# One fp32 transformer block on one core: rotary tables of the queries alone, weight sums from step 10, one context sum put first, and the last group's final sum in two tiles

## The chip, the cores and the metric

The kernel runs on one core of a Trainium2 chip. The metric is device time in microseconds, median of the runs shown; lower is better. Engines are named as in the profile: PE is TensorE (PEld its weight loads), DVE is VectorE, ACT is ScalarE, POOL is GpSimd and SP is SyncE, which only issues transfers. A line number L1079 is line 1079 of the kernel whose profile is shown; behind the place of an edit the changed kernel's lines stand up to six further down.

## The reference

All inputs and outputs are fp32, and the kernel reaches fp32 precision by splitting numbers. Cut to what matters:

```python
D_MODEL, SEQ, CTX_LEN, HEAD_DIM, N_Q_HEADS, N_KV_HEADS = 2048, 512, 256, 128, 12, 4
h  = modulate(rmsnorm(x, norm_g), shift, scale)         # shift, scale, gate = silu(c) @ w_ada + b_ada
hc = modulate(rmsnorm(ctx, norm_g), shift_c, scale_c)   # 256 context tokens: keys and values alone
kc, vc = rmsnorm(heads(hc @ w_k), k_norm_g), heads(hc @ w_v)
p = h @ w_in                                            # q, k, v, z_a, u_b, z_b, gate_a, gate_b
q = rope(rmsnorm(q, q_norm_g)) * HEAD_DIM ** -0.5
k = rope(rmsnorm(k, k_norm_g))
attn = softmax(q @ cat(k, kc).T) @ cat(v, vc)           # 512 queries, 768 keys, 3 query heads to a key head
y_a = (attn * silu(z_a)) @ w_proj_a
y_b = (fft2(u_b).real * silu(z_b)) @ w_proj_b
out = rmsnorm(x + gate * ((sigmoid(gate_a) * y_a + sigmoid(gate_b) * y_b) @ w_out), final_g)
```

## The kernel before

**One product.** Every number is split in two, hi (rounded, written by ACT, L178) and lo (the rest, subtracted by DVE, L179). `mm3` makes three matmuls of it: hi by hi (L334), lo by hi (L335) and hi by lo (L336).

**One group.** The big products (512 x 2048 by 2048 x 1024 or so) are worked in groups, each as seven half-size products instead of eight, in the order P1, Q5, P2, Q6, P7, Q3, Q4. They use the sums A11, Z5, A12, S2, S3, S4 and A22 of the tokens' quarters and weights that are sums of quarters as well (L272). A product has four pieces of weights. It runs into an accumulator in PSUM: "a" and "c" are pairs of banks with the tag x, "b" has the tag y. Between products DVE and ACT subtract the accumulators into the SBUF tiles X, Y and V (`sub`, L1079), and `done` passes a finished quarter on. In the last group of the input projection (LAST, number 7) the final sum is Y = accumulator − Y after Q4, half of the columns at a time.

**The stages.** Start, up to about 137 us: adaLN's vectors (L562, with weights wa that SP's queue loads), the norms of the tokens, the first weights, and the rotary tables. Then the Fourier mixing, the eight groups of the input projection (kinds qz, qz, qz, gate, gate, kv, gate, gate) up to 815 us, attention from 815.7 to about 1010, branch A's groups (10 and 11), and the output groups 8 and 9 up to the end.

**The tables.** `load_rope` loads the rotary table into the form S3's space and the gains of q and k into Z5's. `rotations` multiplies the table by the gains twice, once for queries and once for keys (four DVE operations, L740), into other parts of S3 and Z5, and POOL's queue stores both in `rot_d` (L743). `load_rotations` brings one or the other back into `turning`: that of the queries ahead of the groups, that of the keys at the KV group's P1.

**The context.** The 256 context tokens' keys and values are made in the KV group (number 5) with the same weights: `self.more` puts six matmuls into "y" after each twelve of the group, and at a product's end `more.end` does the context's own subtractions into cxe and ev (L1225).

**Attention** has 48 steps, one for each head and each 128 queries. A step makes scores over 768 keys, their maximum (DVE, L1480), the exponential (ACT, L1482), six transposes (PE, L1498) into one set of banks, a split of these into pth and ptl (ACT copies, DVE subtracts), the division (L1491 and L1492) and the values (256 columns; two transposes L1513, copy L1523, L1524). Into the gaps go products of branch B and at the end the first of branch A, which read weights that were loaded before (filler, DVE L1446). At the steps in SUM_AT, POOL's queue runs a chain of transfers that adds weights of branch A (`weight_sum`).

**What sets the order.** In the start stage the order on PE, ACT and DVE is written by hand. From there on a scheduler orders the instructions of each engine by its own estimates; names of tiles and the buffers that they get come from the program, and waits follow from these. Transfers stay in the order of their queue.

Of the kernel before, what the change touches and what calls it, by code (L numbers as in the profile page):

```python
# [10 lines left out]
F32 = mybir.dt.float32  # L11
F32R = mybir.dt.float32r
ACT = mybir.ActivationFunctionType
ALU = mybir.AluOpType
# [4 lines left out]
P = 128  # L19
# [4 lines left out]
HD = 128  # L24
# [40 lines left out]
NQZ, KV = 3, 5  # L65
# [24 lines left out]
CHUNKS = (0, 2, 1, 3)  # L90
BRANCH_A, BRANCH_B = 10, (6, 7)
A_CHUNKS = ((0, 2), (1, 3))
SUM_AT = (13, 16, 19, 25, 28, 31)
CHAIN_FROM = {BRANCH_A + 1: 3, 8: 2, 9: 2}
A_FORM = {p[0]: (p[1],) for p in PRODUCTS} | {"Q4": ("A12", "A22"), "P2": ()}

# [24 lines left out]
def block_kernel(ctx, tc, xT, ctx_rows, ctx_toks, x, c_row, w_ss, w_gate, vecs, qkg, rope, dft_c, dft_s,  # L121
                 w_start, w_g, w_pab, w_o, final_g, out):
    nc = tc.nc
# [17 lines left out]
    k_d = dsc.tile([NKV, P, KT, HD], F32, name="k_d")  # L141
    cf_d = dsc.tile([4, P, 7, 2, P], F32, name="cf_d")
    v_d = dsc.tile([NKV, P, KT, HD], F32, name="v_d")
    rot_d = dsc.tile([2, P, 2, 4, HD], F32, name="rot_d")
    p7_d = dsc.tile([2, 3, P, 1024], F32, name="p7_d")
    qz_d = dsc.tile([NH, P, 2, 4, HD], F32, name="qz_d")
    b_d = dsc.tile([2, P, 2, T], F32, name="b_d")
# [581 lines left out]
    def load_rope():  # L729
        i = nc.gpsimd.dma_start(by_rows("S3", 0).rearrange("p (a t) d -> p a t d", a=2), rope)  # L730
        with tc.issue_after(i.ins):
            nc.gpsimd.dma_start(by_rows("Z5", 0)[:, 0:4, :], qkg)

    def rotations():

        r, gq = by_rows("S3", 0), by_rows("Z5", 0)
        for i, f in enumerate(("S3", "Z5")):
            o = by_rows(f, 1)
            for a in range(2):
                nc.vector.scalar_tensor_tensor(o[:, 4 * a : 4 * a + 4, :], r[:, 4 * a : 4 * a + 4, :], (HD ** -0.5, 1.0)[i],  # L740
                                               gq[:, None, 2 * i + a, :].broadcast_to([P, 4, HD]),
                                               op0=ALU.mult, op1=ALU.mult)
            nc.gpsimd.dma_start(rot_d[i], o.rearrange("p (a t) d -> p a t d", a=2))  # L743

    def hold():
        held[:] = [None]
# [277 lines left out]
    class Group:  # L1024
# [16 lines left out]
        def steps(self, name):  # L1041

            form, which = next((f, c) for n, f, _, c in PRODUCTS if n == name)
            if name == "Q3" and self.g >= BRANCH_A:
                which = "d"
            start = which not in self.acc
            if start:

                self.acc[which] = Banks() if self.last and which == "c" else pair(self.tags[which])
            a = self.acc[which]  # L1050
            if name == "Q4" and self.last:
                self.finish(a, form)
                return
            if self.more:
                self.more.begin(name)
            for pc in range(self.pieces):
                w = get((name, self.g, pc))

                apart = (self.g, name, pc) in APART
                for i, (k, t) in enumerate((i // 2, i % 2) if not apart else (i % 2, i // 2) for i in range(4)):  # L1060
                    self.mm(a, form, 2 * pc + k, t, w, start and pc == 0 and k == 0,
                            pc == self.pieces - 1 and k == 1, cont=not start)
                    if i % 2:
                        yield
                if self.more:
                    self.more.products(name, which, pc, w, start)
                for f, h, ready in between(self.g, name, pc):
                    if ready:
                        self.forms[f][4 * h : 4 * h + 4] = split_form(whole[f, h])
                    else:  # L1070
                        make_form(f, h)
                job()
                p = None if self.last else context_piece(self.g, name, pc)
                if p:
                    (context_squares if p[0] == "cn" else context_row)(p[1], get(p))
                q = None if self.last else GATE_AT.get((self.g, name, pc))
                if q is not None:
                    use_gate(q, get(("gate", q)), last_split[-1][1])
            sub = lambda o, x, y: nc.vector.tensor_tensor(o, x, y, op=ALU.subtract)  # L1079
            if name == "P1":  # L1080
                self.X = self.new()
                nc.scalar.copy(self.X, a)
            elif name == "Q5":
                self.Y = self.new()
                for t in ((0,), (1,)) if (self.g, name, 3) in APART else ((0, 1),):
                    t = slice(t[0], t[-1] + 1)
                    nc.scalar.copy(self.Y[:, t, :], a[:, t, :])
            elif name == "P2":
                self.done(0, 0, a, None)
            elif name == "Q6":  # L1090
                self.V = self.new()
                sub(self.V, a, self.X)
                sub(self.Y, self.V, self.Y)
                if self.g >= BRANCH_A:
                    sub(self.X, self.V, self.acc["c"])
                    self.done(1, 1, self.X, self.X)
            elif name == "P7" and self.g >= BRANCH_A:
                pass
            elif name == "P7" and self.last:
                for t in range(2):  # L1100
                    sub(self.V[:, t, :], self.V[:, t, :], a[:, t, :])
                self.done(1, 1, self.V, self.V)
            elif name == "P7":
                sub(self.V, self.V, a)
                self.done(1, 1, self.V, self.V)
            elif name == "Q3" and self.g >= BRANCH_A:
                nc.vector.tensor_tensor(self.V, self.V, a, op=ALU.add)
                self.done(0, 1, self.V, self.V)
            elif name == "Q3":
                if not self.last:  # L1110
                    sub(self.X, a, self.X)
                self.done(0, 1, a if self.last else self.X, self.X)
            elif name == "Q4" and self.g == BRANCH_A + 1:
                self.done(1, 0, a, self.Y)
            elif name == "Q4":
                for t in ((0,), (1,)) if (self.g, name, 3) in APART else ((0, 1),):
                    t = slice(t[0], t[-1] + 1)
                    sub(self.Y[:, t, :], a[:, t, :], self.Y[:, t, :])
                self.done(1, 0, self.Y, self.Y)
            if self.more:  # L1120
                self.more.end(name, which)

        def finish(self, a, form):
# [19 lines left out]
    qr = qzp.tile([P, 2048], F32, name="qr")  # L1143
    new_q = lambda: qr[:, :1024].rearrange("p (a h d) -> p a h d", a=2, h=4)
    turning = qr[:, 1024:].rearrange("p (a t d) -> p a t d", a=2, t=4)

    def load_rotations(i, q):
        q.dma_start(turning, rot_d[i])


    sums, stats = small[:, :32], gain.rearrange("p k j -> p (k j)")
# [182 lines left out]
    def next_wide():  # L1334
        turn_wide[0] += 1
        return wide[turn_wide[0] % 3]

    def get_keys(g):
        raw = get(("K", g))
        tk = next_wide() if g else flat(pair("x"))  # L1340
        for t in range(KT):
            nc.tensor.transpose(tk[:, t * P : (t + 1) * P], raw[:, t * P : (t + 1) * P], ident)
        keys = tiles(g)
        split_from(tk[:, :NKEY], *(w[:, :NKEY] for w in keys))
        kv[g] = tuple(keys) + get(("V", g))
# [4 lines left out]
        qs[h] = take((2, T), F32R)  # L1350
        split_from(tq, qs[h][:, 0, :], qs[h][:, 1, :])

    load_rotations(0, nc.gpsimd)
    for g, kind in enumerate(KINDS):
        if g == 3:
            jobs += [lambda: None] * 12 + [context_norm, lambda: None, lambda: None, context_spread]
# [11 lines left out]
        for name in ONE_GROUP:  # L1368
            if (g, name) in ((0, "Q4"), (KV + 1, "P1")):
                assert not any(p[2] == "raw0" for e in ahead for p, _ in e.raws)  # L1370
                load_row(int(g > 0))
            elif (g, name) == (1, "Q5"):
                silu_of_row(0, flat(new_ev()))
            if (g, name) == (0, "P7"):
                raw_pools.remove((rp, 1, "raw0", 1))
            if (g, name) == (0, "Q5"):
                more_hl.append(1)
                look[0] = 4
            elif (g, name) == (KV, "P1"):
                load_rotations(1, nc.scalar)  # L1380
            elif (g, name) == (KV - 1, "Q3"):
                raw_pools.remove((rp, 1, "raw1", 1))
                hl_pools[:] = [p for p in hl_pools if not isinstance(p, int)]
            elif (g, name) == (KV + 1, "Q6"):
                raw_pools += [(rp, 1, "raw1", 1), (gvp, 2, "raw", 2)]
            elif (g, name) == (LAST, "P7"):
                raw_pools.remove((gvp, 2, "raw", 2))
            elif (g, name) == (LAST, "Q3"):

                free += [(fms[i], f"s{i}") for i in (4, 5, 6, 7, 12, 13, 14, 15, 8, 9, 10, 11, 2, 3, 0, 1)]  # L1390
                for h in range(2):
                    load_head(h)
            elif (g, name) == (LAST, "Q4"):
                hl_pools[:] = [p for p in hl_pools if not isinstance(p, int)]
                get_keys(0)
                jobs.append(lambda: turn_queries(0, pair("y")[:, 0, :]))
            group.run(name)
# [613 lines left out]
```

## Time and profile before

| What | Value |
| --- | --- |
| median of the 3 runs shown (lowest, highest) | 1302.36 us (1300.53, 1302.63) |
| profiled execution, its own time | 1303.86 us |
| its span in the profile | 1302.1 us |
| PE busy, share of the span | 1279.2 us, 98% |
| DVE, ACT, POOL busy | 76%, 53%, 13% |
| mean granted clock of TensorE | 0.995 |

Read first how much PE is busy; then its waits, which are short and few; then at each one the timeline, which tells what released it. A timeline row has the start in us, the duration in us, engine, line, operation, out<-in, the count, and in brackets the idle time ahead of it and its releaser. The granted clock is 1.00 where TensorE runs at full speed.

### The profile page before, as it was taken

The numbers are of one execution on the slowest core, as the hardware profiler recorded it, in microseconds if no ns is written. First come the engines' busy times: TensorE is split into PE (matmuls) and PEld (weight loads), VectorE is DVE, ScalarE is ACT, GpSimd is POOL, SyncE is SP. The second block draws the span as 40 slices with busy tenths as digits, with TensorE's granted clock in tenths as the row PEclk, the third lists the DMA queues.
The fourth block names the chain that finished last, engine by engine and source line by source line (L and its number), as shares of the span: only waits on it lengthen the run. The fifth ranks groups of instructions, "written<-read, shape, count | busy, mean of one in ns | idle before, by whom it ended". The sixth has DMA issues, their size and how long they took to land.

```text
span 1302.1 us, 17705 instructions
## 1 busy us (share of the span) xinstructions
PE 1279.2 (98%) x6598; PEld 1052.2 (81%) x6598; DVE 995.7 (76%) x1301; ACT 685.0 (53%) x1076; POOL 169.6 (13%) x223
## 2 busy tenths in 40 slices
PE   8999999999999999999999999999999999999997
PEld 4677988888888888887888888888888888888885
DVE  5667899889679787647687756788889667887676
ACT  5322655545456455444345545666677546464544
POOL 0000011111102111012021010011111211211210
PEclk9999999999999999999999999999999999999998
DMA  9999588988899889977879897477872899998985
GB/s 377 408 381 352 195 223 220 251 219 253 198 315 245 256 282 292 289 198 181 277 203 285 263 234 253 152 227 241 242 237 69 240 246 254 241 210 231 222 203 171
DMA packets 104519, 320.13 MB, mean 246 GB/s; under 512 B 9904, under 2 KB 32944, under 8 KB 100464
## 3 DMA queue, kind: packets, MB, share of 16 engines
q1 hardware_dynamic: 55056, 197.86, 42.1%
q0 software_dynamic: 27200, 98.85, 35.7%
q10 hardware_dynamic: 22176, 22.29, 5.1%
q8 instruction: 52, 0.85, 0.3%
q14 instruction: 35, 0.29, 0.1%
HBM read 283.82 MB, written 35.14 MB: 245 GB/s over the span
## 4 chain that ended last, share of the span: by engine, by line
PE 81%; DMA 8%; DVE 5%; ACT 2%; issue 2%; SPq 0%; ACTq 0%; DVEq 0%
PE banks L334 10%; PE banks L335 10%; PE banks L336 10%; PE x L334 7%; PE x L336 7%; PE x L335 7%; PE y L335 6%; PE y L334 6%; PE y L336 6%; DMA wa<-in_w_ss 3%; PE banks L1498 2%; DMA wr<-in_w_g 2%; PE pd L562 1%; DVE wlo L179 1%; PE pb L334 1%
## 5 line engine op out<-in xcount | busy, mean ns | idle before, releaser
L178 ACT ACTIVATE whi<-R 128x1024 fp32r<-128x1024 f32 x138 | 145.0, 1058 | 137.2 <-PE banks L336 49.1
L179 DVE TENSOR_TENSOR wlo<-R,whi 128x1024 fp32r<-128x1024 f32 x138 | 167.5, 1221 | 51.3 <-ACT whi L178 51.2
L179 DVE TENSOR_TENSOR wlo<-wr,whi 128x1024 fp32r<-128x1024 f32 (+1 forms) x122 | 147.2, 1212 | 70.8 <-ACT whi L178 70.7
L178 ACT ACTIVATE whi<-wr 128x1024 fp32r<-128x1024 f32 (+1 forms) x122 | 127.5, 1051 | 131.2 <-PE y L336 39.2
L334 PE MATMUL banks<-whi,s 128*128 128x512 f32 x396 | 157.4, 398 | 2.4 <-DVE ev L1079 1.5
L335 PE MATMUL banks<-wlo,s 128*128 128x512 f32 x396 | 156.1, 394 | 0.1
L336 PE MATMUL banks<-whi,s 128*128 128x512 f32 x396 | 155.7, 393 | 0.0
L334 PE MATMUL x<-whi,s 128*128 128x512 f32 x352 | 137.2, 390 | 0.0
L336 PE MATMUL x<-whi,s 128*128 128x512 f32 x352 | 137.0, 389 | 0.0
L335 PE MATMUL x<-wlo,s 128*128 128x512 f32 x352 | 136.9, 389 | 0.0
L334 PE MATMUL y<-whi,s 128*128 128x512 f32 x316 | 123.1, 389 | 1.0 <-DVE cxe L1225 1.0
L335 PE MATMUL y<-wlo,s 128*128 128x512 f32 x316 | 123.1, 389 | 0.5 <-DVE wlo L179 0.5
L336 PE MATMUL y<-whi,s 128*128 128x512 f32 x316 | 122.8, 389 | 0.0
L287 POOL DMA_DIRECT2D R<-in_w_g x64 | 56.0, 875 | 413.4 <-DVE wlo L179 241.8
L178 ACT ACTIVATE s<-wr 128x512 fp32r<-128x512 f32 (+2 forms) x93 | 60.3, 677 | 73.6 <-DMA wr<-cf_d 24.0
L179 DVE TENSOR_TENSOR s<-wr,s 128x512 fp32r<-128x512 f32 (+2 forms) x93 | 66.8, 749 | 37.1 <-ACT s L178 36.4
L334 PEld LDWEIGHTS banks<-whi,s 128*128 128x128 f32 x396 | 74.8, 189 | 18.2 <-ACT whi L178 1.9
L336 PEld LDWEIGHTS banks<-whi,s 128*128 128x128 f32 x396 | 74.8, 189 | 15.6
L335 PEld LDWEIGHTS banks<-wlo,s 128*128 128x128 f32 x396 | 74.8, 189 | 14.3 <-DVE wlo L179 0.5
L336 PEld LDWEIGHTS x<-whi,s 128*128 128x128 f32 x352 | 66.1, 188 | 13.9
L334 PEld LDWEIGHTS x<-whi,s 128*128 128x128 f32 x352 | 66.1, 188 | 13.6
L335 PEld LDWEIGHTS x<-wlo,s 128*128 128x128 f32 x352 | 66.1, 188 | 13.5
(321 smaller groups left out, 2826.1 us busy)
## 6 DMA issues: line engine op xcount, KB each, us to landing
wr<-in_w_g SPq DMA_DIRECT2D x128, 512.0 KB, 5.7
R<-in_w_g POOLq DMA_DIRECT2D x64, 512.0 KB, 7.6
wa<-in_w_ss SPq DMA_DIRECT2D x31, 1024.0 KB, 10.2
R<-in_w_g SPq DMA_DIRECT2D x32, 512.0 KB, 5.3
wr<-in_w_gate SPq DMA_DIRECT2D x32, 512.0 KB, 5.1
wr<-in_w_o SPq DMA_DIRECT2D x24, 512.0 KB, 7.2
R<-in_w_o POOLq DMA_DIRECT2D x24, 512.0 KB, 9.2
wr<-in_w_pab SPq DMA_DIRECT2D x20, 512.0 KB, 5.2
```

The source lines that it names most:

```text
L178: first = nc.scalar.activation(hi, src, ACT.Copy)
L179: return first, nc.vector.tensor_tensor(lo, src, hi.bitcast(F32), op=ALU.subtract)
L287: nc.gpsimd.dma_start(chain[e.pc], e.nxt, accum_op=ALU.add)
L334: nc.tensor.matmul(o, ah, bh, start=start, stop=False, skip_group_check=cont)
L335: nc.tensor.matmul(o, ah, bl, start=False, stop=False, skip_group_check=cont)
L336: nc.tensor.matmul(o, al, bh, start=False, stop=stop, skip_group_check=cont)
L562: nc.tensor.matmul(acc[32 * j : 32 * j + 32], c2[:, n, :], w[:, k, :], start=n < 4, stop=n >= KK - 4)
L1498: nc.tensor.transpose(tp[:, k * P : (k + 1) * P], p[:, k * P : (k + 1) * P], ident)
```

## The change

Five edits, of which none takes a matmul away:

1. SUM_AT is earlier: the six chains start at steps 10 to 28 instead of 13 to 31.
2. `rotations` makes the table of the queries alone, in place, from half of the gains, and stores that. At the KV group's P1, ACT's queue loads the raw table and two rows of gains, and at its Q5 two DVE operations (`scale_tables`) make the keys' table of them, behind the last split.
3. At the KV group's Q6 the context's subtraction is called right behind V, ahead of Y.
4. In the group LAST the accumulator "c" is two tiles (`Banks`) instead of one. P7's subtraction goes by halves; the first half of Y is subtracted in Q4's last piece, right after that half's products.
5. The first transposes of the keys (`get_keys`, g = 0) go to a pair of banks with the tag y instead of x.

```diff
-SUM_AT = (13, 16, 19, 25, 28, 31)
+SUM_AT = (10, 13, 16, 19, 25, 28)
...
-    rot_d = dsc.tile([2, P, 2, 4, HD], F32, name="rot_d")
+    rot_d = dsc.tile([P, 2, 4, HD], F32, name="rot_d")
...
-            nc.gpsimd.dma_start(by_rows("Z5", 0)[:, 0:4, :], qkg)
+            nc.gpsimd.dma_start(by_rows("Z5", 0)[:, 0:2, :], qkg[:, 0:2, :])
+    def scale_tables(r, gains, factor):
+        for a in range(2):
+            nc.vector.scalar_tensor_tensor(r[:, a], r[:, a], factor, gains[:, None, a, :].broadcast_to([P, 4, HD]),
+                                           op0=ALU.mult, op1=ALU.mult)
     def rotations():
-        r, gq = by_rows("S3", 0), by_rows("Z5", 0)
-        for i, f in enumerate(("S3", "Z5")):
-            o = by_rows(f, 1)
-            for a in range(2):
-                nc.vector.scalar_tensor_tensor(o[:, 4 * a : 4 * a + 4, :], ...)
-            nc.gpsimd.dma_start(rot_d[i], o.rearrange("p (a t) d -> p a t d", a=2))
+        r = by_rows("S3", 0).rearrange("p (a t) d -> p a t d", a=2)
+        scale_tables(r, by_rows("Z5", 0), HD ** -0.5)
+        nc.gpsimd.dma_start(rot_d, r)
...
-                self.acc[which] = Banks() if self.last and which == "c" else pair(self.tags[which])
+                self.acc[which] = Banks() if (self.last or self.g == LAST) and which == "c" else pair(self.tags[which])
...
+                    if i == 1 and (self.g, name) == (LAST, "Q4") and apart:
+                        nc.vector.tensor_tensor(self.Y[:, 0, :], a[:, 0, :], self.Y[:, 0, :], op=ALU.subtract)
...
             elif name == "Q6":
                 sub(self.V, a, self.X)
+                if self.more:
+                    self.more.end(name, which)
                 sub(self.Y, self.V, self.Y)
...
-            elif name == "P7" and self.last:
+            elif name == "P7" and (self.last or self.g == LAST):
...
-                for t in ((0,), (1,)) if (self.g, name, 3) in APART else ((0, 1),):
-                    t = slice(t[0], t[-1] + 1)
-                    sub(self.Y[:, t, :], a[:, t, :], self.Y[:, t, :])
+                if self.g == LAST:
+                    sub(self.Y[:, 1, :], a[:, 1, :], self.Y[:, 1, :])
+                else:
+                    sub(self.Y, a, self.Y)
...
-            if self.more:
+            if self.more and name != "Q6":
                 self.more.end(name, which)
...
-        tk = next_wide() if g else flat(pair("x"))
+        tk = next_wide() if g else flat(pair("y"))
...
             elif (g, name) == (KV, "P1"):
-                load_rotations(1, nc.scalar)
+                nc.scalar.dma_start(turning, rope)
+                nc.scalar.dma_start(new_q()[:, 0, 0:2, :], qkg[:, 2:4, :])
+            elif (g, name) == (KV, "Q5"):
+                with tc.issue_after(last_split[-1][1].ins):
+                    scale_tables(turning, new_q()[:, 0, 0:2, :], 1.0)
```

DVE at the end of the KV group's Q6, before. The first and third rows are V and Y of the group, L1225 is the context's, and L272 adds weights that a transfer brings:

```order
L1079 TENSOR_TENSOR ev_5034<-y_4684,ev_4681 128x1024
L272 TENSOR_TENSOR wr_5066<-R_1335,wr_5066 128x1024
L1079 TENSOR_TENSOR ev_4795<-ev_5034,ev_4795 128x1024
L1225 TENSOR_TENSOR cxe<-y_4575,ev_4576 128x512
L179 TENSOR_TENSOR wlo_5070<-wr_5046,whi_5069 128x1024
L1225 TENSOR_TENSOR ev_4576<-cxe,ev_4576 128x512
L179 TENSOR_TENSOR wlo_5096<-wr_5066,whi_5095 128x1024
```

And now:

```order
L1081 TENSOR_TENSOR ev_5034<-y_4684,ev_4679 128x1024
L272 TENSOR_TENSOR wr_5066<-R_1332,wr_5066 128x1024
L1227 TENSOR_TENSOR cxe<-y_4572,ev_4573 128x512
L1081 TENSOR_TENSOR ev_4795<-ev_5034,ev_4795 128x1024
L1227 TENSOR_TENSOR ev_4573<-cxe,ev_4573 128x512
L179 TENSOR_TENSOR wlo_5070<-wr_5046,whi_5069 128x1024
L179 TENSOR_TENSOR wlo_5096<-wr_5066,whi_5095 128x1024
```

The context's two operations have each moved up one place: the first stands ahead of Y now, the second ahead of a split.

PE where attention ends, before. `s_8399` is the tile of exponentials that the transposes L1498 read, the rows with `s_8257` are score products, `whi_7925` is the filler and `whi_8014` the first product (P1) of branch A:

```order
L335 MATMUL banks<-s_7916,s_8257 128x256
L334 MATMUL banks<-s_7915,s_8257 128x256
L335 MATMUL banks<-s_7916,s_8257 128x256
L336 MATMUL banks<-s_7915,s_8257 128x256
L1498 MATMUL banks<-ident,s_8399 128x128 x4
L336 MATMUL banks<-s_7915,s_8257 128x256
L334 MATMUL banks<-whi_7925,s_6465 128x512
L335 MATMUL banks<-wlo_7926,s_6465 128x512
L336 MATMUL banks<-whi_7925,s_6466 128x512
L1498 MATMUL banks<-ident,s_8399 128x128
L1498 MATMUL banks<-ident,s_8399 128x128
L334 MATMUL banks<-whi_8014,s_6659 128x512
```

And now, where the same tiles have numbers higher by two:

```order
L335 MATMUL banks<-wlo_7928,s_6467 128x512
L336 MATMUL banks<-whi_7927,s_6468 128x512
L334 MATMUL banks<-s_7917,s_8259 128x256
L335 MATMUL banks<-s_7918,s_8259 128x256
L336 MATMUL banks<-s_7917,s_8259 128x256
L1504 MATMUL banks<-ident,s_8401 128x128 x4
L334 MATMUL banks<-whi_8016,s_6661 128x512
L335 MATMUL banks<-wlo_8017,s_6661 128x512
L336 MATMUL banks<-whi_8016,s_6661 128x512
...
L1504 MATMUL banks<-ident,s_8401 128x128
L1504 MATMUL banks<-ident,s_8401 128x128
```

Between the four transposes and the last two there stood one score matmul and three of the filler; now nine matmuls of P1 stand there (three are shown; the rest repeat them).

ACT at the same place, before. `pth_8410` is the copy of a step's transposes, L1482 the exponentials of steps 46 (`s_8427`) and 47 (`s_8475`), `whi_8501` a split of a weight tile:

```order
L178 ACTIVATE pth_8410<-banks 128x6x128
L1492 ACTIVATE s_8100<-s_8100,gain 128x128
L178 ACTIVATE s_8625<-s_7332 128x512
L1523 COPY R_1335<-banks 128x256
L178 ACTIVATE s_8498<-s_7004 128x512
L178 ACTIVATE s_8454<-s_8371 128x512
L178 ACTIVATE whi_8501<-R_1334 128x1024
L1482 ACTIVATE s_8427,gain<-banks,gain 128x768
L1482 ACTIVATE s_8475,gain<-banks,gain 128x768
L178 ACTIVATE pth_8410<-banks 128x6x128
```

And now:

```order
L178 ACTIVATE pth_8412<-banks 128x6x128
L1488 ACTIVATE s_8477,gain<-banks,gain 128x768
L1529 COPY R_1332<-banks 128x256
L178 ACTIVATE s_8500<-s_7009 128x512
L178 ACTIVATE whi_8503<-R_1331 128x1024
L1488 ACTIVATE s_8429,gain<-banks,gain 128x768
L178 ACTIVATE s_8456<-s_8373 128x512
L178 ACTIVATE pth_8412<-banks 128x6x128
```

The exponential of step 47 has moved from behind that of 46, and from behind the split of the weight tile, to right behind the first of the two copies.

More of the change, by code (lines that the diff above doesn't have):

```diff
@@ L731, in load_rope @@
         with tc.issue_after(i.ins):
-            nc.gpsimd.dma_start(by_rows("Z5", 0)[:, 0:4, :], qkg)
-    def rotations():
-        r, gq = by_rows("S3", 0), by_rows("Z5", 0)
-        for i, f in enumerate(("S3", "Z5")):
-            o = by_rows(f, 1)
-            for a in range(2):
[L740 to L743, printed above, removed]
+            nc.gpsimd.dma_start(by_rows("Z5", 0)[:, 0:2, :], qkg[:, 0:2, :])
[3 more added lines that the diff above has]
+                                           op0=ALU.mult, op1=ALU.mult)
+    def rotations():
+        r = by_rows("S3", 0).rearrange("p (a t) d -> p a t d", a=2)
+        scale_tables(r, by_rows("Z5", 0), HD ** -0.5)
+        nc.gpsimd.dma_start(rot_d, r)
     def hold():
@@ L1145, in block_kernel @@
     turning = qr[:, 1024:].rearrange("p (a t d) -> p a t d", a=2, t=4)
-    def load_rotations(i, q):
-        q.dma_start(turning, rot_d[i])
     sums, stats = small[:, :32], gain.rearrange("p k j -> p (k j)")
@@ L1351, in turn_queries @@
         split_from(tq, qs[h][:, 0, :], qs[h][:, 1, :])
-    load_rotations(0, nc.gpsimd)
+    nc.gpsimd.dma_start(turning, rot_d)
     for g, kind in enumerate(KINDS):
```

## The prediction

> **What bounds the kernel now.** I read the page first, then the waits of TensorE over the whole span, then the timeline around each of its longer waits, and last the windows around the longest. Page, busy time by engine and the chain that ended last:
>
> ```profile
> PE 1279.2 (98%) x6598; PEld 1052.2 (81%) x6598; DVE 995.7 (76%) x1301; ACT 685.0 (53%) x1076; POOL 169.6 (13%) x223
> ```
>
> ```profile
> PE 81%; DMA 8%; DVE 5%; ACT 2%; issue 2%; SPq 0%; ACTq 0%; DVEq 0%
> ```
>
> TensorE is busy for 98% of the span and makes up 81% of the chain. No edit takes a matmul away, so only its waits, and time in which it runs slowly, can go. The waits of TensorE (engine and line, who released it: us in total, times, longest):
>
> ```profile
> PE banks L1498 <- ACT s L1482: 2.0, 1, 2.0
> PE pd L562 <- DMA wa<-in_w_ss: 1.5, 3, 0.5
> PE banks L334 <- DVE ev L1079: 1.5, 1, 1.5
> ```
>
> ```profile
> PE y L334 <- DVE cxe L1225: 1.0, 1, 1.0
> PE banks L334 <- ACT s L1482: 0.7, 2, 0.4
> ```
>
> Four of these lie where the change works: wa (early stage, beside the tables' DMA), cxe (context's Q6), ev (the last group's final sum) and s L1482 (the end of attention). Together that is some 6 us. A change of 0.2% is 2.6 us here, about what a measurement of this kernel can tell from no change.
>
> **Part 1, tables of the queries alone.** Timeline of TensorE at two of the adaLN products that are 64 matmuls long; the first is broken by a load:
>
> ```profile
> 93.50 2.80 PE L562 MATMUL pd<-wa,c 128*32 128x256 f32 x48
> 96.81 1.07 PE L562 MATMUL pd<-wa,c 128*32 128x256 f32 x16 [0.52 <-DMA wa<-in_w_ss]
> ```
>
> ```profile
> 109.39 3.66 PE L562 MATMUL pd<-wa,c 128*32 128x256 f32 x64
> ```
>
> The broken one takes 96.81 + 1.07 − 93.50 = 4.38 us, the whole one 3.66: the wait costs 0.72. What that load shared the DMA engines with (DMA of 78 to 100 us; issues with KB each and us to landing):
>
> ```profile
> DMA packets 1440, 8.03 MB, mean 365 GB/s; under 512 B 162, under 2 KB 162, under 8 KB 759
> ```
>
> ```profile
> rot_d<-S POOLq DMA_DIRECT2D x1, 512.0 KB, 5.0
> rot_d<-Z POOLq DMA_DIRECT2D x1, 512.0 KB, 9.9
> ```
>
> The store of the keys' table (Z) goes, and with it half of the gains, which were loaded earlier. 512 KB over the mean of this stretch (365 GB/s) is 1.4 us of DMA time that the load has to itself, twice the wait; I take the 0.72 off whole (bounds 0 and 1.4). Also gone are two of the four DVE operations at L740, and the rest now write in place:
>
> ```profile
> 77.48 1.29 DVE L740 SCALAR_TENSOR_TENSOR S<-S,Z 128x512 f32<-128x512 f32 x2
> ```
>
> ```profile
> 79.06 0.54 POOL L743 DMA_DIRECT2D rot_d<-S  x1 [17.66 <-DVE S L740]
> ```
>
> ```profile
> 89.77 0.42 DVE L638 TENSOR_TENSOR S<-xt 128x256 f32<-128x256 f32 x1
> ```
>
> That is 1.29 us of DVE, off the path here (no matmul is released by L740): nothing. In-place writing makes form_row's first write (L638 at 89.77) wait for the store of S. Issued at 79.06 and landed after 5.0, the store is done at 84.1, 5.7 us ahead; even with Z's 9.9 it would be done at 89.0. Nothing. The same two operations return in the KV group, in a gap of DVE (timeline of DVE):
>
> ```profile
> 566.67 1.23 DVE L179 TENSOR_TENSOR wlo<-R,whi 128x1024 fp32r<-128x1024 f32 x1 [2.07 <-ACT whi L178]
> ```
>
> The order puts them ahead of this split: 1.29 us into 2.07 of idle time. Without that cover a weight tile's lo half would be 1.29 us later. ACT's queue issues one DMA more, past P1's splits; an issue of this kind takes POOL 0.54 above, and nothing waits for its data before Q5, a product later. Nothing for both.
>
> **Part 2, context's Q6 in front.** Timeline of DVE and then of TensorE:
>
> ```profile
> 611.62 1.23 DVE L272 TENSOR_TENSOR wr<-R,wr 128x1024 f32<-128x1024 f32 x1 [0.58 <-DMA wr<-in_w_g]
> 612.77 1.22 DVE L1079 TENSOR_TENSOR ev<-ev,ev 128x1024 f32<-128x1024 f32 x1
> 613.90 0.68 DVE L1225 TENSOR_TENSOR cxe<-y,ev 128x512 f32<-128x512 f32 x1
> ```
>
> ```profile
> 614.64 0.50 PE L334 MATMUL y<-whi,s 128*128 128x512 f32 x1 [1.03 <-DVE cxe L1225]
> ```
>
> TensorE waits for cxe, and cxe stands behind a 1.22 us operation that nobody on TensorE needs. Swapped, cxe starts at 612.77 and ends at about 613.45; the y matmul, now placed two matmuls earlier, starts at about 613.55, and those two follow it. A matmul here takes 0.226 from one to the next:
>
> ```profile
> 200.00:300.00 100.00, 100.00 (x442) 1.00 0.86 244
> ```
>
> (100 us with 442 matmuls.) The two that used to stand ahead of the wait take 0.45 behind it, so the work done by 614.64 is 614.64 − 613.55 − 0.45 = 0.64 further on: I take 0.7 (bounds 0, if the load that L272 waits for is later by as much, and the whole 1.03). The context's first subtraction now holds the 1.22 us one back by 0.7; what it makes is read after the product, and no matmul waits for it.
>
> **Part 3, the last sum in two tiles.** Timelines of DVE and of TensorE:
>
> ```profile
> 812.67 1.23 DVE L179 TENSOR_TENSOR wlo<-wr,whi 128x1024 fp32r<-128x1024 f32 x1 [1.49 <-ACT whi L178]
> 814.29 1.29 DVE L1079 TENSOR_TENSOR ev<-x,ev 128x512 f32<-128x512 f32 x2 [0.40 <-PE x L336]
> ```
>
> ```profile
> 815.73 0.47 PE L334 MATMUL banks<-whi,s 128*128 128x512 f32 x1 [1.47 <-DVE ev L1079]
> ```
>
> Both halves (1.29 together) are subtracted only after the last matmul, and attention's first matmul waits for both. Now the first half is complete six matmuls (1.36 us) earlier; DVE is free at about 813.85 (operations in a row start some 0.1 before the end of the one ahead, as at 613.90 above), subtracts it until about 814.5, and the second half runs from there to 815.15. With the 0.15 from DVE's end to the matmul that the rows show (814.29 + 1.29 to 815.73), TensorE starts at about 815.25 to 815.3 instead of 815.73: 0.5 (bounds 0 and 1.0, the wait less one half's 0.6 or so). The keys' transposes in "y" change nothing: that tile was read out one group before.
>
> **Part 4, the sums from step 10, and the order of attention.** The sums are six chains of DMAs on POOL, off the path. What they change is which buffer each later step gets, and with that the order that the scheduler writes over the last 20 steps on three engines. The stall there is the kernel's longest. TensorE and ACT around it:
>
> ```profile
> 1000.35 0.82 PE L1498 MATMUL banks<-ident,s 128*128 128x128 f32 x6
> ```
>
> ```profile
> 1007.28 0.44 PE L1498 MATMUL banks<-ident,s 128*128 128x128 f32 x2 [2.03 <-ACT s L1482]
> 1008.16 0.67 PE L334 MATMUL banks<-whi,s 128*128 128x512 f32 x1 [0.44 <-ACT s L1482]
> ```
>
> ```profile
> 1000.94 0.63 ACT L178 ACTIVATE s<-s 128x512 fp32r<-128x512 f32 x1
> 1001.46 0.81 ACT L178 ACTIVATE pth<-banks 128x768 fp32r<-128x768 f32 x1
> ...
> 1005.29 1.06 ACT L178 ACTIVATE whi<-R 128x1024 fp32r<-128x1024 f32 x1 [0.35 <-PE banks L336]
> 1006.25 0.88 ACT L1482 ACTIVATE s<-banks,gain 128x768 f32<-128x768 f32 x1
> ...
> 1007.13 0.89 ACT L1482 ACTIVATE s<-banks,gain 128x768 f32<-128x768 f32 x1
> ```
>
> TensorE waits for two exponentials (steps 46 and 47) that run one after the other behind a split of 1.06 us: 2.03 + 0.44 = 2.47 us. In the new order the scores of 47 are finished before the values of 43, so its exponential follows the copy of step 44's transposes directly, and nine matmuls of the branch's P1 stand before the two transposes that need the other one. I walk it with the durations above; each time in the walk is an estimate. In the new order two splits stand before step 44's copy, so I put it at 1002.2 rather than 1001.46; exponential 47 then ends at about 1003.9, before TensorE comes to P1, which I put at 1005.0 behind the values that changed places. Nine matmuls of 0.226 last until 1007.05; copy, split and the 1.06 us split run until 1005.9, exponential 46 until 1006.8. The stall is gone, with 0.2 us to spare; a later wait for step 45's copy leaves 0.4. And the stall costs more than itself (window of TensorE: us, busy, granted clock, DMA share, GB/s):
>
> ```profile
> 1008.00:1012.00 4.00, 3.84 (x10) 0.57 0.38 22
> ```
>
> After it the granted clock averages 0.57 over four microseconds: 4 x 0.43 = 1.7 us lost. So 2.5 + 1.7 − 0.4 = 3.8 off. Against it I set 0.7 for new small waits in the reordered steps (the 0.4 and 0.3 that attention shows elsewhere now), with bounds of 0 and 4.2, one more stall of the old size.
>
> The Trainium skill, page TensorE: Matmul & The Clock Gate, Part 1: The HAM clock gate, says that the clock halves after an idle window of about 3.4 us, and its summary advises against gaps over about 3. By that rule a gap of 2.5 us would not halve it; the trace shows that it did, and I go by the trace. By the rule alone the 1.7 would stay and the sum be smaller by that.
>
> **Part 5, given back.** The branches that follow load almost without pause (window of TensorE with the DMA share, then ACT and TensorE's weight loads):
>
> ```profile
> 1030.00:1160.00 130.00, 129.41 (x599) 1.00 0.96 241
> ```
>
> ```profile
> 1124.16 1.06 ACT L178 ACTIVATE s<-wr 128x1024 fp32r<-128x1024 f32 x1 [4.03 <-DMA wr<-in_w_o]
> ```
>
> ```profile
> 1127.48 0.19 PEld L335 LDWEIGHTS banks<-wlo,s 128*128 128x128 f32 x1 [0.48 <-DVE wlo L179]
> ```
>
> At 1127.48 TensorE already has no slack: one load late by 1 us makes it wait 1 us. The load is issued when TensorE has freed its buffer, so it moves along with TensorE; I give back 0.5 (bounds 0 and 3.8).
>
> **The sum** against the profiled execution, 1303.86 us (span 1302.1): 0.7 + 0.7 + 0.5 + 3.8 − 0.7 − 0.5 = 4.5 off, 1299.4. The median of the runs shown is 1302.36, so I forecast 1302.36 − 4.5 = 1297.9.
>
> **The rivals.** (1) The end of attention keeps a stall of its size. Between ready and needed lie only 0.2 us in my walk, and any split of 0.6 us that comes later undoes it. Then parts 1 to 3 remain, less 0.2 for later waits: 1302.4 − 1.7 = 1300.7. (2) The gain of attention is given back to the loads of the branches; for it the DMA share of 0.96, against it that loads follow TensorE. 1302.4 − 1.9 + 0.7 = 1301.2. (3) Slower: transposes become the bound of the last steps. There is one set of banks for them, so each step is transposes (0.82), copy (0.81) and this subtraction in series (groups of instructions):
>
> ```profile
> L179 DVE TENSOR_TENSOR ptl<-banks,pth 128x768 fp32r<-128x768 f32 x48 | 45.8, 954 | 12.0 <-ACT pth L178 11.6
> ```
>
> That is 2.6 us of about 4 (48 steps from 815.7 to 1010). The new order on ACT puts an exponential (0.88) and one to two splits (0.63) before that copy; from 1.4 us in front of it on, TensorE waits. Four steps with 1.2 us each, with the half clock of 1.7 after and the old stall's 2.5 + 1.7 in another place, come to 1302.4 − 1.9 − 4.2 + 4.8 + 1.7 + 4.2 = 1307.0. For it: three engines are reordered over 20 steps. Against: ACT idles in this stage between its groups. (4) The clock: if the halving comes from something else than the gap, the 1.7 stay: 1297.9 + 1.7 = 1299.6. For it, that the gap is short; against it, that the clock is whole before the gap and halved right behind it. The rule cited in part 4 would give this case. (5) The change does none of it: the waits reappear one operation on. 1302.4.
>
> **The numbers.** Forecast 0.46; rival 1 0.21; rival 2 0.09; rival 3 0.13; rival 4 0.05; rival 5 0.06. Faster by over 0.2% (below 1299.8): nearly all of the forecast (0.43), the smaller half of rival 4 (0.03), and 0.06 where rivals 1 and 2 come out better than their number: 0.52. Slower (above 1305.0): rival 3, 0.13, and 0.03 of rivals 1, 2 and 5 with a further stall of 4.2: 0.16. Within: 0.32. Below the forecast the bounds of parts 1 to 3 (1.4 + 1.0 + 1.0 against 1.9 taken) and the 1.2 of small waits could bring 2.7 more; I reach down to 1294.9. Upwards the range goes through rivals 1, 2 and 5 to 1305.3 and leaves out most of rival 3. The forecast's own range is 1295.5 to 1300.
>
> **What would show it.** Right: no wait of L1504's transposes on an exponential over 1 us near 1000, a granted clock of 1.00 in the 20 us after, the y matmul waiting under 0.5 us near 612, attention's first matmul under 1.1 us, and no wait on wa near 96. Wrong: any wait of TensorE over 1.5 us between 930 and 1010, or waits on loads in the branches that sum to over 2 us. If attention stalls as now, the forecast is wrong by its largest term; if the early waits stay, only by 2 us.

## The result, and the profile after

The changed kernel takes 1297.12 us (median of 6 runs, 1296.16 to 1297.93) against 1302.92 (median of 6 runs, 1300.53 to 1305.16) before: 5.8 us less, a ratio of 0.9954 with a 95% interval of 0.9943 to 0.9964. The forecast was 1297.9. The profiled execution has a span of 1294.4 us against 1302.1.

The page of the changed kernel, busy time by engine, and the waits of TensorE (us in total, times, longest):

```profile
PE 1276.4 (99%) x6598; PEld 1050.6 (81%) x6598; DVE 994.9 (77%) x1302; ACT 684.6 (53%) x1076; POOL 169.1 (13%) x222
```

```profile
PE pd L543 <- DVE s L541: 3.2, 3, 2.4
PE pc L523 <- DVE eps_t L346: 1.1, 1, 1.1
PE banks L334 <- DVE ev L1081: 1.0, 1, 1.0
PE pd L562 <- DMA wa<-in_w_ss: 0.7, 2, 0.5
...
PE banks L1504 <- DVE ptl L179: 0.4, 1, 0.4
PE banks L334 <- ACT s L1488: 0.4, 1, 0.4
```

The first two rows are waits of the start stage that lie at none of the edits (2.9 and 1.0 before). Of the four waits at the edits, the longest, 2.0 on an exponential, is gone, and the one on cxe is too short to be listed. The wait for the last group's sum went from 1.5 to 1.0, that on wa from 1.5 to 0.7 in all. Now the places one by one. The adaLN product that was broken, and the context's Q6 on DVE and on TensorE:

```profile
93.16 3.66 PE L562 MATMUL pd<-wa,c 128*32 128x256 f32 x64
```

```profile
610.82 0.68 DVE L1227 TENSOR_TENSOR cxe<-y,ev 128x512 f32<-128x512 f32 x1
611.42 1.21 DVE L1081 TENSOR_TENSOR ev<-ev,ev 128x1024 f32<-128x1024 f32 x1
```

```profile
611.14 0.39 PE L336 MATMUL x<-whi,s 128*128 128x512 f32 x1
611.56 0.50 PE L334 MATMUL y<-whi,s 128*128 128x512 f32 x1
```

The product is whole and takes 3.66 us. The context's subtraction stands ahead of the 1.21 us one, and the y matmul follows the x one 0.42 us after its start, where 0.23 is the pace: 0.2 of waiting is left of 1.03. The last group's final sum and attention's first matmul:

```profile
811.14 0.68 DVE L1064 TENSOR_TENSOR ev<-x,ev 128x512 f32<-128x512 f32 x1
811.74 0.68 DVE L1081 TENSOR_TENSOR ev<-x,ev 128x512 f32<-128x512 f32 x1
```

```profile
812.57 0.47 PE L334 MATMUL banks<-whi,s 128*128 128x512 f32 x1 [0.98 <-DVE ev L1081]
```

The first half (L1064) starts right when DVE is free, the second 0.60 later, as in the walk. And the end of attention, on ACT, on TensorE, and as a window of TensorE (us, busy, granted clock, DMA share, GB/s):

```profile
999.00 0.81 ACT L178 ACTIVATE pth<-banks 128x768 fp32r<-128x768 f32 x1
1000.16 0.90 ACT L1488 ACTIVATE s<-banks,gain 128x768 f32<-128x768 f32 x1 [0.36 <-DVE s L179]
...
1002.96 0.90 ACT L1488 ACTIVATE s<-banks,gain 128x768 f32<-128x768 f32 x1
```

```profile
1002.12 0.47 PE L334 MATMUL banks<-whi,s 128*128 128x512 f32 x1
...
1004.28 0.38 PE L1504 MATMUL banks<-ident,s 128*128 128x128 f32 x2
```

```profile
1004.00:1008.00 4.00, 4.00 (x21) 1.00 0.35 30
```

The exponential of step 47 ends at 1001.06, and P1 starts at 1002.12 without a wait. That of 46 ends at 1003.86, and the two transposes behind the nine matmuls start at 1004.28 without a wait, with 0.4 us to spare. The clock stays at 1.00.

**Where the time came from.** Both traces have the same 6598 matmuls, so the start of the n-th in the one less its start in the other tells how far ahead the changed kernel is. A column of the table is what this lead grows by in a stretch (us; the stretches are in times of before), for the kernels of the experiments too, all against the one profiled execution of before:

| Kernel | 88-105 (wa) | 417-432 | 432-599 | 599-623 (Q6) | 782-818 (last sum) | 818-990 | 990-1037 (end of attention) | 1037-1292 |
| --- | --- | --- | --- | --- | --- | --- | --- | --- |
| the change | 0.73 | 0.83 | -0.31 | 1.00 | 0.53 | -0.61 | 4.57 | 0.50 |
| sums alone | 0.12 | 0.74 | -1.75 | 0.31 | 0.03 | -0.27 | 4.45 | 0.08 |
| all but sums | 0.73 | 0.83 | -0.47 | 0.67 | 0.54 | -0.48 | 1.57 | 0.31 |
| sums from 10, last at 31 | 0.37 | -0.25 | -0.15 | 0.15 | 0.04 | -0.41 | -0.07 | 0.46 |
| no tables | 0.44 | 0.83 | -0.01 | 0.91 | 0.54 | -0.37 | 4.56 | -0.72 |
| no Q6 | 0.73 | 0.83 | -0.10 | 0.10 | 0.51 | -0.56 | 4.61 | -0.31 |
| no two tiles | 0.73 | 0.83 | -0.45 | 1.00 | 0.03 | -1.04 | 4.42 | 0.32 |
| last sum at 25 | 0.73 | 0.37 | -0.88 | 1.12 | 0.53 | -1.46 | 4.55 | -0.49 |

Not all of a column is an edit's. The two profiles of before and of the change are 7.7 us apart, where the medians are 5.8 apart. In 432-599 the sums alone lose 1.75, although their edit lies elsewhere, and between 105 and 417, which the table leaves out, three kernels (all but sums, no Q6, last sum at 25) lose 0.7 to 1.2 and the others nothing. At 990 the orders differ, so a few tenths can belong to the column beside.

### The profile page after: what moved, and what is told of

Same layout as the page of the kernel before. It is cut to its first block, busy times and chain, and to the rows that moved or that the text cites. A ratio compares the mean times of both kernels' runs of the same rounds, so it can differ in the third digit from the quotient of the medians.

```text
span 1294.4 us, 17700 instructions
## 1 busy us (share of the span) xinstructions
PE 1276.4 (99%) x6598; PEld 1050.6 (81%) x6598; DVE 994.9 (77%) x1302; ACT 684.6 (53%) x1076; POOL 169.1 (13%) x222
## 4 chain that ended last, share of the span: by engine, by line
PE 95%; DMA 2%; DVE 1%; ACT 1%; issue 0%; SPq 0%; ACTq 0%; DVEq 0%
PE banks L334 10%; PE banks L335 10%; PE banks L336 10%; PE x L336 9%; PE x L334 9%; PE x L335 9%; PE y L334 8%; PE y L335 8%; PE y L336 8%; PE banks L1504 2%; PE pd L562 2%; PE pb L334 2%; PE pb L335 1%; PE pb L336 1%; PE pc L334 1%; PE pc L336 1%
```

## The experiments

**1. Sums alone** (kernel before, one line):

```diff
-SUM_AT = (13, 16, 19, 25, 28, 31)
+SUM_AT = (10, 13, 16, 19, 25, 28)
```

> The kernel before with SUM_AT alone changed. The theory (the sums give attention its new order, and that takes the long stall and the half clock behind it away): faster than before by 3.1 to 4.9 us, no wait of TensorE over 1 us between 930 and 1010, a granted clock of 1.00 there; the waits on cxe (1.0) and on the last group's sum (1.5) stay. The rival (the earlier parts carry the gain, attention's is given back to the loads of the branches): within 1 us of before.

Measured: 1299.20 against 1303.31, 4.1 us less, ratio 0.9963 (0.9951 to 0.9976). Here and below the microseconds are differences of medians, and the ratio is the recorded one, not their quotient; before has runs of its own beside each set of experiments, the change has none. Window of TensorE over the place of the stall:

```profile
1004.00:1014.00 10.00, 10.00 (x65) 1.00 0.29 23
```

No stall, no half clock; the theory's 3.1 to 4.9 holds, and the rival is out. The waits on cxe (0.7 here) and on the last sum (1.5) are there as before.

**2. All but the sums** (the changed kernel):

```diff
-SUM_AT = (10, 13, 16, 19, 25, 28)
+SUM_AT = (13, 16, 19, 25, 28, 31)
```

> The changed kernel with the old SUM_AT. The theory: 1.5 to 2.5 us faster than before (tables 0.7, context's Q6 0.7, last sum 0.5 to 0.65), and the stall of 2.0 + 0.4 us at attention's end stays, with or without half clock behind it. The rival: 4 us or more faster than before.

Measured: 1301.03, 2.3 us less than before, ratio 0.9981 (0.9970 to 0.9993). The stall is there, and this time the clock did not fall (TensorE's timeline, and windows):

```profile
1006.55 0.44 PE L1504 MATMUL banks<-ident,s 128*128 128x128 f32 x2 [2.03 <-ACT s L1488]
1007.43 0.50 PE L334 MATMUL banks<-whi,s 128*128 128x512 f32 x1 [0.44 <-ACT s L1488]
```

```profile
1005.42:1008.83 3.41, 1.83 (x8) 1.00 0.49 37
1008.83:1012.25 3.42, 3.42 (x26) 1.00 0.53 32
```

So the halving does not always follow this stall. By the table's 990-1037 column, the same stall without it costs 1.57 us less than in the profile of before, which had it: the price of the half clock, forecast at 1.7. The two parts add up within the noise: 4.1 and 2.3, against 5.8 for both.

**3. Earlier sums, but the last chain left at step 31** (kernel before):

```diff
-SUM_AT = (13, 16, 19, 25, 28, 31)
+SUM_AT = (10, 13, 16, 19, 25, 31)
```

> The kernel before with the sums at steps 10, 13, 16, 19, 25 and 31: earlier but for the last chain. Theory A (the last chain's step alone sets the order at the end, by the buffers it holds): within 1 us of before, with the stall of 2.0 + 0.4 us. Theory B (it counts that the chains as a whole run earlier, through the transfers): 2 to 4 us faster than before.

Measured: 1303.80 against 1303.31, ratio 1.0000 (0.9991 to 1.0009). The instructions of TensorE, ACT and DVE stand in the order of before, and the stall is back, with half clock behind it:

```profile
1007.30 0.44 PE L1498 MATMUL banks<-ident,s 128*128 128x128 f32 x2 [2.03 <-ACT s L1482]
1008.18 0.50 PE L334 MATMUL banks<-whi,s 128*128 128x512 f32 x1 [0.45 <-ACT s L1482]
```

Theory A holds as to the step: moving the five other chains alone does nothing. This kernel and that of experiment 1 differ only in the last chain: with it at step 28 attention has the new order, with it at 31 the old one. Whether the chain acts by the buffer that it holds for three steps, as the theory says, or by the places of its transfers, no run here tells apart.

**4. Both tables at the start again** (the changed kernel; `load_rope`, `rotations` and the load ahead of the groups as before, too):

```diff
-    rot_d = dsc.tile([P, 2, 4, HD], F32, name="rot_d")
+    rot_d = dsc.tile([2, P, 2, 4, HD], F32, name="rot_d")
...
-                nc.scalar.dma_start(turning, rope)
-                nc.scalar.dma_start(new_q()[:, 0, 0:2, :], qkg[:, 2:4, :])
-            elif (g, name) == (KV, "Q5"):
-                with tc.issue_after(last_split[-1][1].ins):
-                    scale_tables(turning, new_q()[:, 0, 0:2, :], 1.0)
+                load_rotations(1, nc.scalar)
```

> The changed kernel with both tables made and stored at the start, as before. The theory: 5.8 - 0.7 = 5.1 us faster than before, 0.7 slower than the change, with a wait on wa of 0.5 us at about 96 us back. The rival (the tables do nothing, that wait came and went by itself): as fast as the change, 5.8 us faster than before, and no such wait.

Measured: 1298.18, 5.1 us less than before, ratio 0.9955 (0.9942 to 0.9967), which is too wide to tell 0.7 us. The trace does tell (adaLN's product):

```profile
93.25 3.94 PE L562 MATMUL pd<-wa,c 128*32 128x256 f32 x64
```

In all five traces with the new tables this product takes 3.66 us whole. In all four without, the load is late: 3.94 here, 4.38 before, and a lead in the stretch that is smaller by 0.73 (before), 0.61 (sums alone), 0.36 (sums from 10) and 0.29 (here), in the mean 0.5. The wait is real and its size changes from run to run; the full 0.72 was the case of one profile.

**5. Gaps of TensorE by themselves** (the changed kernel; behind its end, 56 times with k from 2 to 8 and n from 40 to 54; the loop's body):

```diff
+                for i in range(n):
+                    nc.tensor.matmul(acc, w, m, start=i == 0, stop=i == n - 1)
+                nc.vector.tensor_copy(c[:, 0:256], acc[:, 0:256])
+                for _ in range(k):
+                    nc.vector.tensor_tensor(c[:, 0:256], c[:, 0:256], one[:, 0:256], op=ALU.subtract)
+                nc.scalar.copy(m[:, 0:16], c[:, 0:16])
```

> The changed kernel with 56 made gaps of TensorE behind its end: runs of 40 to 54 matmuls, and between them a chain of 3 to 9 operations on DVE and one on ACT for which the next matmul waits, so gaps of an estimated 1.5 to 3.5 us. Its time isn't compared. Theory G (the length of one gap decides): sorted by length, the gaps that are followed by half clock lie above one length between 1.4 and 2.5 us, the rest below. Theory W (TensorE's busy share in stretches of 3.41 us, on a grid that runs through the whole execution, decides): gaps of about 2 us have both outcomes, and they are told apart by how much of the grid's stretch was idle, with the boundary at about half. Theory P (the rule of 3.4 us idle): no half clock behind any gap under 3.4 us.

Measured, in one execution: gaps of 1.82 to 4.58 us in steps of 0.46. Half clock followed 4 of 8 gaps of 1.82, 5 of 8 of 2.28, 7 of 8 of 2.74, of 3.20 and of 3.66, and all of the longer ones. The stretches of half clock last 3.41 us or multiples of it, and start on one grid of 3.41 us. Two gaps of the same length (timeline), and the grid's windows around them (us, busy, clock):

```profile
1620.26 12.32 PE L1956 MATMUL sw_acc<-sw_m,sw_w 128*128 128x512 f32 x46 [1.82 <-ACT sw_m L1960]
...
1730.04 11.18 PE L1956 MATMUL sw_acc<-sw_m,sw_w 128*128 128x512 f32 x48 [1.81 <-ACT sw_m L1960]
```

```profile
1617.13:1620.55 3.42, 1.60 (x7) 1.00 0.00 0
1620.55:1623.96 3.41, 3.41 (x9) 0.50 0.00 0
1726.36:1729.78 3.42, 1.87 (x9) 1.00 0.00 0
1729.78:1733.19 3.41, 3.15 (x14) 1.00 0.02 5
```

The first gap lies in one window, of which TensorE was busy for 1.60; the next window runs at half clock. The second is shared by two windows, neither busy for less than 1.87; the clock stays. Over all windows at full clock: 38 that were busy for under 1.47 us were all followed by half clock, and none of the 144 that were busy for 1.75 or more; of the 9 between, 5 were. Theory W holds, but for a band at the boundary that it doesn't explain; G falls, since the length alone does not decide. P falls too: 4 gaps of 1.82 us were enough, and one of 3.66, shared by two windows, was not. The Trainium skill, page TensorE: Matmul & The Clock Gate, Part 1: The HAM clock gate, states a free-running window of 3413 ns. The grid agrees with that. An idle window is not needed here; one that is busy for less than about half will do.

The stall of the kernel follows the same rule. Before, and sums from 10 with the last at 31:

```profile
1004.92:1008.33 3.41, 0.94 (x5) 1.00 0.35 32
1008.33:1011.75 3.42, 3.42 (x9) 0.50 0.36 20
```

```profile
1005.94:1009.35 3.41, 1.61 (x7) 1.00 0.52 41
1009.35:1012.76 3.41, 3.41 (x13) 0.50 0.29 29
```

Busy for 0.94 and 1.61, both followed by half clock (1.61 lies in the band where either can follow); with 1.83 in experiment 2 it was not. Laying a pattern of 2.03 us idle, 0.44 busy and 0.44 idle over the grid in every phase, with the boundary at 46% busy, gives half clock in 64% of the phases (an estimate from these rows).

**6. Context's Q6 behind Y again** (the changed kernel):

```diff
-                if self.more:
-                    self.more.end(name, which)
                 sub(self.Y, self.V, self.Y)
...
-            if self.more and name != "Q6":
+            if self.more:
```

> The changed kernel with the context's subtraction of Q6 behind Y again. The theory: 0.7 us slower than the change, 5.1 faster than before, and the wait on cxe of about 1 us back. The rival (what that wait holds up is made good later by the loads): as fast as the change.

Measured: 1298.44 against 1302.98, 4.5 us less than before, ratio 0.9962 (0.9949 to 0.9976). TensorE's wait is back:

```profile
613.81 0.50 PE L334 MATMUL y<-whi,s 128*128 128x512 f32 x1 [0.90 <-DVE cxe L1225]
```

In the table's column the five kernels with the edit are ahead by 0.67 to 1.12 (mean 0.94), the four without by 0 to 0.31 (mean 0.14): 0.8 us. That 1.3 us were lost in the median goes beyond the edit's 0.8 and lies inside the interval.

**7. One tile for the last group's sum** (the changed kernel; P7's halves and the keys' "y" put back as well):

```diff
-                self.acc[which] = Banks() if (self.last or self.g == LAST) and which == "c" else pair(self.tags[which])
+                self.acc[which] = Banks() if self.last and which == "c" else pair(self.tags[which])
...
-                    if i == 1 and (self.g, name) == (LAST, "Q4") and apart:
-                        nc.vector.tensor_tensor(self.Y[:, 0, :], a[:, 0, :], self.Y[:, 0, :], op=ALU.subtract)
...
```

> The changed kernel with the last group's accumulator in one tile and both halves subtracted behind the last matmul (the keys' transposes to x again). The theory: 0.5 us slower than the change, 5.3 faster than before, attention's first matmul waits 1.5 instead of 1.0. The rival (attention has slack on its other engines and makes it good): as fast as the change.

Measured: 1298.11, 4.9 us less than before, ratio 0.9964 (0.9951 to 0.9976). Attention's first matmul:

```profile
813.73 0.47 PE L334 MATMUL banks<-whi,s 128*128 128x512 f32 x1 [1.47 <-DVE ev L1079]
```

Five traces with the edit are ahead by 0.51 to 0.54 in that stretch, four without by 0 to 0.04: 0.5 us, and the same each time. Here, too, the medians alone could not tell. The keys' "y" went back with the rest; by itself it was not tried.

**8. One place earlier still** (the changed kernel):

```diff
-SUM_AT = (10, 13, 16, 19, 25, 28)
+SUM_AT = (7, 10, 13, 16, 19, 25)
```

> The changed kernel with the sums at steps 7, 10, 13, 16, 19 and 25, one place earlier still. If any order without the long stall does, the same as the change within 1 us. If the order is a matter of luck with the buffers, a new stall of 1 to 4 us is as likely as not, and the time is 1 to 5 us above the change. Faster than the change by over 1 us isn't expected, since only 1.6 us of waits are left in attention.

Measured: 1299.12 against 1302.98, 3.9 us less than before, ratio 0.9965 (0.9952 to 0.9978). The end of attention is as good as the change's, but its first steps have a new stall (timeline of TensorE):

```profile
826.83 0.87 PE L1504 MATMUL banks<-ident,s 128*128 128x128 f32 x6 [1.54 <-DVE ptl L179]
```

Transposes wait for the subtraction that empties their one set of banks, and that subtraction is late itself (timeline of DVE, and of POOL's queue):

```profile
825.82 0.96 DVE L179 TENSOR_TENSOR ptl<-banks,pth 128x768 fp32r<-128x768 f32 x1 [1.73 <-DMA g_d<-ev]
```

```profile
814.02 0.88 POOL L1630 DMA_DIRECT2D s<-in_w_pab  x1 [5.22 <-DMA s<-in_w_pab]
```

DVE is idle for 1.73 us until a store of the gates (`g_d`) has landed. This is a late transfer and not rival 3 of the prediction, where the series of transposes, copy and subtraction is the bound: ACT's copy was done 2.6 us earlier. The store took 10.0 us from issue to landing here, and 6.8 to 8.2 in the nine other traces, where it landed before DVE came to the subtraction (in the change 0.3 us before). What runs beside it here alone is the first chain's adding transfer, from 814.02 to 825.3; in the change the first chain starts at 833. That this transfer slows the store is argued from these times. The profiled execution is the slowest of the five runs, 1300.07, and two of them, 1296.61 and 1297.33, are as fast as the change, so the stall need not come each time. No version here beats the change.

## Why the prediction was right

**Tables: 0.7 taken, 0.5 found.** The step was right, its size was that of one execution. In one detail the walk was wrong: the keys' table is scaled ahead of another split than the one named (timeline of DVE):

```profile
556.17 1.29 DVE L737 SCALAR_TENSOR_TENSOR qr<-qr 128x512 f32<-128x512 f32 x2
557.37 1.22 DVE L179 TENSOR_TENSOR wlo<-R,whi 128x1024 fp32r<-128x1024 f32 x1
```

It stands three splits earlier than forecast, at a place with less cover (0.85 us of idle time there in the profile of before), and no wait of TensorE follows there.

**Q6: 0.7 taken, 0.8 found. Last sum: 0.5 taken, 0.5 found.**

**Attention: 3.8 taken; 4.6 in the profile, some 4 in the mean.** At this place the changed kernel is 2.65 us ahead (the matmul of the same number starts at 1004.63 before and at 1001.98 now; the orders differ here, so this holds to some tenths). With that added, the walk's four times can be laid beside the trace: exponential 47 done at 1003.7 (walked 1003.9), P1 at 1004.8 (1005.0), exponential 46 done at 1006.5 (1006.8), the two transposes at 1006.9 (1007.05). Behind the first, two misses cancel: step 44's copy starts 0.55 earlier than walked (999.00 + 2.65 against 1002.2), and the exponential does not follow it directly but waits 0.36 us for a split on DVE. Three sizes were off. The 0.4 that was to be left as a later wait is not there. And the 1.7 of half clock (1.6 measured) was taken as certain because the one profile had it: it comes only when the grid of 3.41 us falls badly, in 2 of the 3 traces with the stall. In the column the stall gave 4.5 − 1.6 = 2.9, which is 0.4 more than its two waits; where that comes from is not resolved. With 2.9 for the stall and 64% of 1.6 behind it, the mean is 3.9. That this is so near the 3.8 is in part luck. Less the two losses that follow, it gives 3.3 for the sums alone; they measured 4.1, with an interval of 3.1 to 6.4.

**New small waits: 0.7 taken, 0.1 to 0.3 found.** In the column 818-990 the new order is 0.27 to 1.04 behind in five kernels (mean 0.57; the sixth has the stall of experiment 8). But the two kernels with the old order are 0.41 and 0.48 behind as well: much of it is that the profile of before was lucky there.

**Given back: 0.5 taken, not resolved.** In the column 1037-1292, the six kernels without the stall run from −0.72 to 0.50 (mean −0.10), the three with it from 0 (before) to 0.46 (mean 0.26). The difference, 0.4, has the forecast's sign and is smaller than the scatter.

**The rivals.** Rival 1 (a stall of the old size stays) is out by the window at 1.00. Rival 2 (the gain is given back to the loads) is out by the branches' column. Rival 3 did not come about in any of the six kernels with the new order: the stall of experiment 8 is a late store. Rival 4 (the halving has another cause than the gap) is out by the made gaps, though what decides is the window and not the gap's length. Rival 5 is out by the traces.

The sum is 0.5 + 0.8 + 0.5 + 3.9 − 0.2 − 0.4 = 5.1. Measured: 5.8, with an interval of 4.7 to 7.4 (0.9964 and 0.9943 of 1302.92). Against this sum the forecast of 4.5 was low chiefly for the small waits that it set against the gain. The other 0.7 up to 5.8 no term accounts for; it lies inside the interval. The time came out nearer than the gain (0.8 off against 1.3) because the median of before is 1302.92 over six runs and not 1302.36: that is luck. Two bounds were loose: 1.4 for the tables is more than the whole wait of 0.72, and the terms named for the lower end of the range, 2.7, give 1295.2 and not 1294.9. One more difference between the two profiles belongs to no edit: 0.8 us at 417 to 432, a late weight split in the profile of before, which is gone in six of the eight other traces, whatever they change.

## What to carry to other kernels

A stall at the end of a stage can hang on transfers that TensorE never waits for, by way of the scheduler's order: moving six chains took 4 us away, and moving all but the last of them did nothing. A wait of some tenths that shows in one profile should be looked for in several before its size is used; edits worth 0.5 us don't show in medians that scatter by 3 us, but they show as the same lead in every trace that has them. And a gap on TensorE should be priced with the clock behind it, as a chance.

## What was not expected of the hardware

TensorE's granted clock is set by windows of 3.41 us on a fixed grid: after a window in which it was busy for less than about half (all 38 under 1.47 us; none of 144 with 1.75 or more) the next runs at 0.50. In the nine other traces no window goes against this. The same gap of 1.82 us had half clock behind it in 4 of 8 cases. A stall of 2.5 us therefore costs 2.5 in one execution and 4.1 in another (with the 1.6 of experiment 2), which fits the wider scatter of the kernel before (1300.53 to 1305.16) beside the change's (1296.16 to 1297.93). The mean clock, which is on record for each run, has the same sign: 0.9957 in the mean over 55 runs of the three kernels with the stall, 0.9971 over 31 runs of the six without. It also holds the half clock at the kernel's start and end, which differs from run to run, so that the stall's half clock makes the scatter is not shown.
